# An encoder layer on one core: x^T laid out by the host, q rotated before the row scales are known

## The chip, the cores and the metric

The kernel runs on one core of one Trainium2 chip. The metric is the device time in microseconds (us), the median of several runs. Inputs are float32; each matrix product is made from two rounded parts of each factor, an upper part (hi) and a rest (lo), so that the products hold nearly full precision.

## The reference, cut to what matters

```python
h = rms_norm(x, norm_mix_pre)                     # x is [256, 2048]
proj = einsum('bsd,dc->bsc', h, w_in)             # 2048 x 10240
qa, ka, va, qn, kn, vn, gates = split(proj)
qa, ka = apply_rope(qa), apply_rope(ka)           # per token, per head of 128
oa = diff_attention(qa, ka, va, lam)              # softmax(q k^T / sqrt(128)), two maps per head
on = neighbourhood_attention(qn, kn, vn, na_rpb)
...
y = mixed @ w_out;  x = x + rms_norm(y, ...)      # then a squared-ReLU MLP, 2048 -> 8192 -> 2048
```

The norm divides each token (row of x) by the root of its mean square. Since that is one factor per token, it can be put on after the product: the kernel multiplies x times the gain with the weights, and puts the row scales on q, k and v later. The rotation (rope) is linear in its input, and the softmax of a score takes any factor of a query's row as its scale.

## The kernel before, in words

All of x's normed transpose, hT, stays in SBUF: 16 tiles of [128 channels, 256 tokens hi | 256 tokens lo]. The weights stream through in groups of 512 columns, and a group in four chunks of 1 MiB (four tiles of 128 rows each). `load` issues a chunk on the SP queue into a buffer "raw" (three of them, in turn); `split` makes hi on ScalarE (CAST, L115) and lo on VectorE (TENSOR_TENSOR, L116), in two halves, into three hi and three lo buffers. A raw buffer is free when the lo part is made, a hi or lo buffer when TensorE has used it.

`wgroup` makes 512 columns transposed, four PSUM banks of 128 columns (L191 for hi times both parts, L192 for lo times hi); `agroup` makes v, with tokens on partitions (L229 to L231). Four PSUM banks serve these in turn: a bank of q must be read out before k's can take it, a bank of k before v's. The first groups are q (qa), k (ka) and v (va) of the first two differential heads, then the same for the next two, and so on to the gates, the projections and the MLP. The order on each engine is made by a scheduler when the program is built.

At the start x comes in four blocks of [256 tokens, 512 columns], between the chunks of q's weight. `x_parts` transposes it on TensorE (L268, 32 transposes), and ScalarE and VectorE make hi and lo of it times the gain, from PSUM (L273, L274). `x_squares` sums the squares of each block on ScalarE (L345). `row_scales` then makes rx, the factor of each token: as a column, times 1/sqrt(128) (rxs), and, through two products with ones on TensorE (L78), as a row on all partitions (rxb), by which the tables cosT and sinT are multiplied. `rope_evac` adds the two halves of a bank (L254 on ScalarE copies one half, L256 on VectorE adds), which frees the bank, and rotates with the scaled tables (L385 to L388). So q, k and v all come out scaled. `diff_head` scores a head (ds) and applies the exponential with the scale 1/sqrt(128).

`small_inputs` loads the tables, the four lambda vectors (lq), subln, mask and g_mlp; before, it stands in the postlude, behind the last chunk of q. Loads take eight semaphores in turn, DMAHW0 to DMAHW7. A load that comes to one of them waits in the queue until the earlier load with it has landed, and all that stands behind it on SP waits too.

Of the kernel before, what the change touches and what calls it, by code (L numbers as in the profile page):

```python
# [14 lines left out]
ALU = mybir.AluOpType  # L15
# [23 lines left out]
def encoder_layer(ctx: ExitStack, tc: tile.TileContext, a, out):  # L39
# [32 lines left out]
    def along_tokens(r, b, name):  # L72
        """r [P tokens, token tile] as a row of all tokens, on all partitions."""
        ps = bank(f"{name}_p")
        for t in range(2):
            dg = t1k(f"{name}_d{t}")
            nc.vector.tensor_scalar_mul(dg[:, :P], ident, r[:, t : t + 1])
            nc.tensor.matmul(ps[:, t * P : (t + 1) * P], ones, dg[:, :P], start=True, stop=True)  # L78
        nc.scalar.copy(b, ps[:, :T])

    def inv_rms(ss, n, name, r=None):
        """(ss / n + eps) ** -0.5, per partition."""
# [9 lines left out]
    last_load = [None]  # L92

    def load(src, k0, nk, c0, cw, name):
        """Rows k0*128.. of a weight: [P, nk, cw]."""
# [5 lines left out]
    def split(raw, name, pieces=2, after=()):  # L101
        """Two float32r parts whose sum is raw. after[s] are instructions that go ahead of piece s."""
# [28 lines left out]
    x = a["x"]  # L131
    xv = x.rearrange("(t p) c -> p t c", p=P)
    xp = []
    first = []
    for i in range(4):
        xt = page([P, 2, 512], F32, f"x_{i}")
        xi = xv[:, :, i * 512 : (i + 1) * 512]
        xp.append(xt)
        if i == 0:
            raw = wp.tile([P, 4, 512], F32, tag="raw", name="first0_w")  # L140
            view = a["w_in"][: 4 * P, QA : QA + 512].rearrange("(k p) c -> p k c", p=P)
            for h in range(2):
                cs = slice(h * 256, (h + 1) * 256)
                nc.sync.dma_start(xt[:, :, cs], xi[:, :, cs])
                for k in range(h * 2, h * 2 + 2):
                    nc.sync.dma_start(raw[:, k], view[:, k])
            first.append(raw)
        else:
            nc.sync.dma_start(xt, xi)
            if i < 3:  # L150
                first.append(load(a["w_in"], i * 4, 4, QA, 512, f"first{i}"))
# [20 lines left out]
    def advance(n):  # L172
        """Trace the next n stages of the attention heads that wait for their turn, and one chore."""
# [9 lines left out]
    def wgroup(src, c0, act, nk, evac, name, first=(), hook=None, mid=None, after={}, k_first=False, inner=None):  # L183
        """out^T of 512 columns: weights stationary. act(k) is [P, hi 256 | lo 256]."""
# [35 lines left out]
    def agroup(src, c0, stat, nk, evac, name, tail=1, between=None):  # L220
        """out of 512 columns: activations stationary. stat(k, t) is (hi, lo) of [P, 128].
        The last ``tail`` chunks go token tile by token tile; between(i) may trace instructions
        ahead of the i-th of the second tile's products there and returns the last of them."""
# [27 lines left out]
    def halves(ps, name):  # L251
        """The sum of the two halves of a bank, in SBUF."""
# [7 lines left out]
    hT = [page([P, 2, 512], F32R, f"hT{i}") for i in range(8)]  # L260

    def x_parts(i):
        """The transpose of four tiles of x times the gain, in two parts [P, hi | lo]."""
        acts = []
        for k in range(i * 4, i * 4 + 4):
            pt = bank(f"hT_t{k}")
            for t in range(2):
                nc.tensor.transpose(  # L268
                    pt[:, t * P : (t + 1) * P], xp[i][:, t, (k % 4) * P : (k % 4 + 1) * P], ident
                )  # L270
            d = hT[k // 2][:, k % 2]
            g = g_pre[:, k : k + 1]
            acts.append(nc.scalar.activation(d[:, :T], pt[:, :T], AF.Copy, scale=g).ins)  # L273
            nc.vector.scalar_tensor_tensor(  # L274
                d[:, T:], pt[:, :T], g, d[:, :T].bitcast(F32), op0=ALU.mult, op1=ALU.subtract
            )

# [18 lines left out]
    ssx = const.tile([P, 8], F32, name="ssx")  # L296

# [22 lines left out]
    # Position bias: row (h, i) of rpbp holds the bias of row offset i - 3 at column offsets  # L320
    # -63..63. Each is written 64 times at a pitch of 127 and read at a pitch of 126.
# [20 lines left out]
    def x_squares(i):  # L342
        for t in range(2):
            j = junk512("jx0").rearrange("p a b -> p (a b)")
            nc.scalar.activation(  # L345
                j, xp[i][:, t], AF.Square, accum_out=ssx[:, t * 4 + i : t * 4 + i + 1]
            )

    def postlude():
        with tc.issue_after(last_load[0]):  # L350
            small_inputs()
        row_scales()
        head_constants()

    def prelude(ch):
# [3 lines left out]
        if ch >= 2:  # L359
            x_squares(ch - 2)  # L360
        if ch == 3:
            x_squares(2)
            x_squares(3)
        return [[]] + [acts[i : i + 1] for i in range(3)] if ch == 0 else None

# [8 lines left out]
    def product3(ps, stat, s_at, mov, m_at, start, stop):  # L374
        """ps (+)= stat^T @ mov, each given in two parts."""
# [43 lines left out]
    def p_transposed(p, name):  # L419
        """[P queries, (t, keys)] -> [P keys, (key tile, queries)]"""  # L420
# [12 lines left out]
    def diff_head(h, qT, kT, v, hl):  # L433
        p = t2k(f"dp{h}")
        for t in range(2):
# [16 lines left out]
            nc.vector.tensor_scalar_mul(nbs, nb, SCALE)  # L452
            e = t2k(f"de{h}{t}")
            z = small(2, f"dz{h}{t}")
            for c in range(2):
# [5 lines left out]
                    scale=SCALE,  # L461
# [108 lines left out]
    head = dict(first=first, hook=prelude, mid=postlude, k_first=True)  # L570
    for kind in ("a", "n"):
        for half in range(2):
# [7 lines left out]
            wgroup(w_in, kc + off, hmov, KD, kev(kT), f"k{nm}")  # L580
            agroup(w_in, vc + off, hstat, KD, v_evac(v), f"v{nm}")
            if kind == "a":
                pending += [diff_head(half * 2 + hl, qT, kT, v, hl) for hl in range(2)]
# [289 lines left out]
```

## Time and profile before

| | |
|---|---|
| median of three runs | 1396.07 us (1395.98 to 1398.43) |
| span of the profiled execution, first to last instruction | 1394.5 us |
| TensorE (PE) busy | 1374.6 us, 99% |
| VectorE (DVE) busy | 835.8 us, 60% |
| ScalarE (ACT) busy | 668.7 us, 48% |
| HBM traffic | 191 GB/s over the span |

The profiled execution has no time of its own beside the span; the span is 1.6 us under the median. Times in rows are us from the span's start. Matmuls overlap in the pipe: a row's length is that of one from its start to its modelled end, and the distance between starts is what one costs. In the list of waits the columns are: who waited, for whom, us in total, times, longest.

### The profile page before, as it was taken

The numbers are of one execution on the slowest core, as the hardware profiler recorded it, in microseconds if no ns is written. First come the engines' busy times: TensorE is split into PE (matmuls) and PEld (weight loads), VectorE is DVE, ScalarE is ACT, GpSimd is POOL, SyncE is SP. The second block draws the span as 40 slices with busy tenths as digits, with TensorE's granted clock in tenths as the row PEclk, the third lists the DMA queues.
The fourth block names the chain that finished last, engine by engine and source line by source line (L and its number), as shares of the span: only waits on it lengthen the run. The fifth ranks groups of instructions, "written<-read, shape, count | busy, mean of one in ns | idle before, by whom it ended". The sixth has DMA issues, their size and how long they took to land.

```text
span 1394.5 us, 17896 instructions
## 1 busy us (share of the span) xinstructions
PE 1374.6 (99%) x7240; PEld 1177.8 (84%) x7240; DVE 835.8 (60%) x1155; ACT 668.7 (48%) x1023; POOL 7.9 (1%) x19
## 2 busy tenths in 40 slices
PE   7999999999999999999899999999999999999997
PEld 6888888888888888888788888888888888888886
DVE  6868866676656565654755555555575554444445
ACT  7554554545444445543744444444464543334332
POOL 0000000000000000000000000000000000000000
PEclk9999999999999999999999999999999999999999
DMA  9674755564555555675455565656555556555551
GB/s 317 202 214 154 202 177 173 171 191 155 165 205 182 203 181 183 203 279 184 149 182 181 182 193 170 211 170 200 189 196 185 203 186 227 195 187 205 181 199 73
DMA packets 117490, 265.16 MB, mean 190 GB/s; under 512 B 15008, under 2 KB 16288, under 8 KB 109216
## 3 DMA queue, kind: packets, MB, share of 16 engines
q1 hardware_dynamic: 117264, 264.03, 57.3%
q8 instruction: 56, 0.92, 0.3%
q14 instruction: 26, 0.21, 0.0%
q10 hardware_dynamic: 144, 0.01, 0.0%
HBM read 261.92 MB, written 3.92 MB: 191 GB/s over the span
## 4 chain that ended last, share of the span: by engine, by line
PE 98%; DVE 1%; DMA 0%; ACT 0%; SPq 0%; issue 0%; DVEq 0%; POOLq 0%; POOL 0%; ACTq 0%
PE u_p L191 17%; PE u_p L192 9%; PE acc L779 8%; PE acc L778 8%; PE acc L777 8%; PE gb_p L191 4%; PE ga_p L191 4%; PE qa_p L191 2%; PE gb_p L192 2%; PE ga_p L192 2%; PE ka_p L191 2%; PE qn_p L191 2%; PE bb_p L191 2%; PE ba_p L191 2%; PE kn_p L191 2%; PE y_p L229 2%
## 5 line engine op out<-in xcount | busy, mean ns | idle before, releaser
L191 PE MATMUL u_p<-h2T,u_h 128*128 128x512 f32 x1024 | 359.9, 398 | 0.5 <-DVE r_m L85 0.5
L192 PE MATMUL u_p<-h2T,u_l 128*128 128x256 f32 x1024 | 284.3, 280 | 0.0
L116 DVE TENSOR_TENSOR d_l<-d_w,d_h 128x1024 fp32r<-128x1024 f32 x128 | 151.1, 1221 | 164.2 <-ACT d_h L115 163.7
L116 DVE TENSOR_TENSOR u_l<-u_w,u_h 128x1024 fp32r<-128x1024 f32 x128 | 151.1, 1222 | 146.0 <-ACT u_h L115 144.7
L191 PEld LDWEIGHTS u_p<-h2T,u_h 128*128 128x128 f32 x1024 | 192.0, 189 | 45.5 <-DVE r_m L85 0.9
L115 ACT CAST d_h<-d_w 128x1024 fp32r<-128x1024 f32 x128 | 128.3, 1052 | 191.1 <-PE acc L779 187.5
L778 PE MATMUL acc<-d_l,uh 128*128 128x512 f32 x512 | 199.0, 389 | 0.0
L779 PE MATMUL acc<-d_h,ul 128*128 128x512 f32 x512 | 198.9, 389 | 0.0
L777 PE MATMUL acc<-d_h,uh 128*128 128x512 f32 x512 | 198.2, 389 | 0.0
L192 PEld LDWEIGHTS u_p<-h2T,u_l 128*128 128x128 f32 x1024 | 193.8, 189 | 1.3
L115 ACT CAST u_h<-u_w 128x1024 fp32r<-128x1024 f32 x128 | 128.0, 1049 | 123.9 <-PE u_p L191 62.5
L778 PEld LDWEIGHTS acc<-d_l,uh 128*128 128x128 f32 x512 | 96.1, 188 | 20.1
L777 PEld LDWEIGHTS acc<-d_h,uh 128*128 128x128 f32 x512 | 96.1, 188 | 20.0
L779 PEld LDWEIGHTS acc<-d_h,ul 128*128 128x128 f32 x512 | 96.1, 188 | 19.8
L191 PE MATMUL gb_p<-hT,gb_h 128*128 128x512 f32 x256 | 90.4, 398 | 0.0
L191 PE MATMUL ga_p<-hT,ga_h 128*128 128x512 f32 x256 | 90.0, 397 | 0.0
L192 PE MATMUL gb_p<-hT,gb_l 128*128 128x256 f32 x256 | 71.4, 281 | 0.0
L192 PE MATMUL ga_p<-hT,ga_l 128*128 128x256 f32 x256 | 70.3, 280 | 0.0
L191 PEld LDWEIGHTS gb_p<-hT,gb_h 128*128 128x128 f32 x256 | 47.9, 188 | 11.5
L116 DVE TENSOR_TENSOR gb_l<-gb_w,gb_h 128x1024 fp32r<-128x1024 f32 x32 | 37.8, 1221 | 31.1 <-ACT gb_h L115 31.1
L191 PEld LDWEIGHTS ga_p<-hT,ga_h 128*128 128x128 f32 x256 | 47.4, 188 | 10.5
L116 DVE TENSOR_TENSOR y_l<-y_w,y_h 128x1024 fp32r<-128x1024 f32 x32 | 37.9, 1222 | 27.8 <-ACT y_h L115 27.8
(213 smaller groups left out, 2348.1 us busy)
## 6 DMA issues: line engine op xcount, KB each, us to landing
u_w<-in_w_up SPq DMA_DIRECT2D x64, 1024.0 KB, 5.4
d_w<-in_w_down SPq DMA_DIRECT2D x64, 1024.0 KB, 4.9
ga_w<-in_w_in SPq DMA_DIRECT2D x16, 1024.0 KB, 5.2
gb_w<-in_w_in SPq DMA_DIRECT2D x16, 1024.0 KB, 5.2
y_w<-in_w_out SPq DMA_DIRECT2D x16, 1024.0 KB, 5.1
ka_w<-in_w_in SPq DMA_DIRECT2D x8, 1024.0 KB, 6.1
va_w<-in_w_in SPq DMA_DIRECT2D x8, 1024.0 KB, 5.2
qn_w<-in_w_in SPq DMA_DIRECT2D x8, 1024.0 KB, 5.1
```

Of the source, the lines that this page charges most:

```text
L115: nc.scalar.copy(hi[part], raw[part])
L116: nc.vector.tensor_sub(lo[part], raw[part], hi[part].bitcast(F32))
L191: nc.tensor.matmul(ps[b], hi[:, k % 4, cs], mv, start=(k == 0), stop=False)
L192: nc.tensor.matmul(ps[b][:, :T], lo[:, k % 4, cs], mv[:, :T], start=False, stop=(k == nk - 1))
L229: nc.tensor.matmul(ps[t], sh, hi[:, k % 4], start=(k == 0), stop=False)
L777: nc.tensor.matmul(acc[t][c], uh[:, k % 4, ts_], hi[:, 0, cs], start=(k == 0), stop=False)
L778: nc.tensor.matmul(acc[t][c], uh[:, k % 4, ts_], lo[:, 0, cs], start=False, stop=False)
L779: nc.tensor.matmul(acc[t][c], ul[:, k % 4, ts_], hi[:, 0, cs], start=False, stop=(k == NK - 1))
```

## The change

The host gives x a second time, transposed and laid out as [128 channels, 16 tiles, 256 tokens] (xT). hT is made from it straight out of SBUF, without transposes. The loads at the start are cut into other pieces and put in the order in which TensorE uses them. x itself is now loaded in the k group, only for the squares; with that the row scales come at the end of the k group. q of the first two heads is rotated with the plain tables, and its scale goes into the exponential of these heads (rxs in place of the constant). k, v and all later groups have scaled tables as before.

```diff
-    for i in range(4):
-        xt = page([P, 2, 512], F32, f"x_{i}")
...
+    nc.sync.dma_start(first[0][:, 0], fv[0][:, 0])
+    nc.sync.dma_start(xT[0][:, 0:1], a["xT"][:, 0:1])
+    nc.sync.dma_start(first[0][:, 1], fv[0][:, 1])
+    nc.sync.dma_start(xT[0][:, 1:4], a["xT"][:, 1:4])
+    for k in range(2, 4):
+        nc.sync.dma_start(first[0][:, k], fv[0][:, k])
+    for i in range(1, 3):
+        nc.sync.dma_start(xT[i], a["xT"][:, i * 4 : i * 4 + 4])
+        for h in range(2):
+            nc.sync.dma_start(first[i][:, h * 2 : h * 2 + 2], fv[i][:, h * 2 : h * 2 + 2])
+    last_load[0] = nc.sync.dma_start(xT[3], a["xT"][:, 12:16]).ins
...
     def x_parts(i):
...
-            pt = bank(f"hT_t{k}")
-            for t in range(2):
-                nc.tensor.transpose(
-                    pt[:, t * P : (t + 1) * P], xp[i][:, t, (k % 4) * P : (k % 4 + 1) * P], ident
-                )
+            src = xT[i][:, k % 4]
...
-            acts.append(nc.scalar.activation(d[:, :T], pt[:, :T], AF.Copy, scale=g).ins)
+            acts.append(nc.scalar.activation(d[:, :T], src, AF.Copy, scale=g).ins)
...
+    def x_rows(i):
+        xt = page([P, 2, 512], F32, f"x_{i}")
+        nc.sync.dma_start(
+            xt, a["x"].rearrange("(t p) c -> p t c", p=P)[:, :, i * 512 : (i + 1) * 512]
+        )
+        xp.append(xt)
...
     def postlude():
-        with tc.issue_after(last_load[0]):
-            small_inputs()
         row_scales()
         head_constants()
...
-        if ch >= 2:
-            x_squares(ch - 2)
+        if ch == 2:
+            with tc.issue_after(last_load[0]):
+                small_inputs()
         if ch == 3:
-            x_squares(2)
-            x_squares(3)
+            with tc.issue_after(last_load[0]):
+                x_rows(0)
...
+    def second(ch):
+        if ch < 3:
+            with tc.issue_after(last_load[0]):
+                x_rows(ch + 1)
+        x_squares(ch)
...
-    def diff_head(h, qT, kT, v, hl):
+    def diff_head(h, qT, kT, v, hl, sc):
...
-            nc.vector.tensor_scalar_mul(nbs, nb, SCALE)
+            nc.vector.tensor_scalar_mul(nbs, nb, sc[t])
...
-                    scale=SCALE,
+                    scale=sc[t],
...
-    head = dict(first=first, hook=prelude, mid=postlude, k_first=True)
+    head = dict(first=first, hook=prelude, k_first=True)
+    head_k = dict(hook=second, mid=postlude)
...
-            wgroup(w_in, kc + off, hmov, KD, kev(kT), f"k{nm}")
+            wgroup(w_in, kc + off, hmov, KD, kev(kT), f"k{nm}", **(head_k if nm == "a0" else {}))
...
+                sc = [rxs[:, t : t + 1] for t in range(2)] if half == 0 else [SCALE] * 2
+                pending += [diff_head(half * 2 + hl, qT, kT, v, hl, sc) for hl in range(2)]
...
+        "xT": f["x"][0].T.reshape(KD, P, T).transpose(1, 0, 2),
```

On the SP queue, before, the fourth chunk of q's weight (qa_3_w) and the first of k's stand among the small inputs; a name in brackets is what a load waits for.

```order
L149 DMA x_105<-in_x 128x2x512 [waits DMAHW3_49]
L98 DMA qa_3_w<-in_w_in 128x4x512 [waits DMAHW5_49,DMAHW6_49,DMAHW4_49,DVE_49]
L160 DMA cosT<-in_cosT 128x256
L161 DMA sinT<-in_sinT 128x256
L164 DMA subln<-in_subln 128x2 [waits DMAHW7_49]
L165 DMA mask<-in_mask 128x64 [waits DMAHW0_49]
L166 DMA g_mlp<-in_g_mlp_pre 128x16 [waits DMAHW1_49]
L98 DMA ka_0_w<-in_w_in 128x4x512 [waits DMAHW2_49,DVE_49]
```

In the changed kernel the same stretch of the SP queue reads as follows; xT_92 is the last quarter of x^T, and sinT is the load that holds DMAHW7.

```order
L148 DMA xT_92<-in_xT 128x1024 [waits DMAHW5_49]
L157 DMA cosT<-in_cosT 128x256 [waits DMAHW6_49]
L158 DMA sinT<-in_sinT 128x256 [waits DMAHW7_49]
L160 DMA lq<-in_lam_q 128x128 [waits DMAHW0_49]
...
L161 DMA subln<-in_subln 128x2 [waits DMAHW4_49]
L162 DMA mask<-in_mask 128x64 [waits DMAHW5_49]
L163 DMA g_mlp<-in_g_mlp_pre 128x16 [waits DMAHW6_49]
L98 DMA qa_3_w<-in_w_in 128x4x512 [waits DMAHW7_49,DVE_49]
L98 DMA ka_0_w<-in_w_in 128x4x512 [waits DMAHW0_49,DVE_49]
L293 DMA x_299<-in_x 128x2x512 [waits DMAHW1_49]
L98 DMA ka_1_w<-in_w_in 128x4x512 [waits DMAHW2_49,DVE_49]
```

All nine small inputs now stand ahead of qa_3_w, and the first block of x (x_299) ahead of ka_1_w. Further on in the same queue the other three blocks of x stand behind the second chunk of v:

```order
L98 DMA va_0_w<-in_w_in 128x4x512 [waits DMAHW5_49,DMAHW2_49,DVE_49]
L98 DMA va_1_w<-in_w_in 128x4x512 [waits DMAHW6_49,DMAHW3_49,DVE_49]
L293 DMA x_389<-in_x 128x2x512
L293 DMA x_435<-in_x 128x2x512
L293 DMA x_481<-in_x 128x2x512 [waits DMAHW1_49]
L98 DMA va_2_w<-in_w_in 128x4x512 [waits DMAHW4_49,DVE_49]
```

Before, no load of x stood there. The wait of va_1_w for VectorE is for the raw buffer of ka_2.

On ScalarE, at the end of the k group and the start of v, before, the casts of the weights follow each other (qa_128 is q, rope_r the copied half of a bank):

```order
L371 CAST qa_128<-rope_s 128x256 x3
L115 CAST ka_3_h<-ka_3_w 128x1024 x2
L115 CAST va_0_h<-va_0_w 128x1024 x2
L115 CAST va_1_h<-va_1_w 128x1024 x2
L254 COPY rope_r<-ka_p_469 128x256
```

In the changed kernel the squares of the last blocks of x (jx, with the sum in ssx) stand between them:

```order
L301 ACTIVATE jx_483,ssx<-x_435 128x512
L301 ACTIVATE jx_485,ssx<-x_435 128x512
L115 CAST ka_3_h<-ka_3_w 128x1024 x2
L301 ACTIVATE jx_527,ssx<-x_481 128x512
L301 ACTIVATE jx_529,ssx<-x_481 128x512
L115 CAST va_0_h<-va_0_w 128x1024 x2
L115 CAST va_1_h<-va_1_w 128x1024 x2
```

On VectorE, before, the lo parts of the same chunks stood in one row ahead of the addition for k's first bank (ka_p_469). In the changed kernel the work on the row scales stands among them; ka_p_385 is k's first bank now, whose buffer v's first bank takes:

```order
L116 TENSOR_TENSOR ka_3_l<-ka_3_w,ka_3_h 128x1024 x2
L307 TENSOR_REDUCE sx<-ssx 128x2
L85 TENSOR_SCALAR rx_m<-sx 128x2
L319 TENSOR_REDUCE ls<-lv 128x2
L116 TENSOR_TENSOR va_0_l<-va_0_w,va_0_h 128x1024
L77 TENSOR_SCALAR rxb_d_553<-ident,rx 128x128
L77 TENSOR_SCALAR rxb_d_556<-ident,rx 128x128
L310 TENSOR_SCALAR rxs<-rx 128x2
L116 TENSOR_TENSOR va_0_l<-va_0_w,va_0_h 128x1024
L116 TENSOR_TENSOR va_1_l<-va_1_w,va_1_h 128x1024 x2
L322 SCALAR_TENSOR_TENSOR lam<-le 128x1
L253 TENSOR_TENSOR rope_s<-ka_p_385,rope_r 128x256
```

What moved here is the sum of the squares and what hangs on it (sx to rxs): before, it stood in the q group. On TensorE the two products for rxb stand between the last product of k and the first of v.

## Rows read from the trace of the kernel before

**Rows 1.** The page: span, and TensorE's busy time and instructions.
```profile
span 1394.5 us, 17896 instructions
...
PE 1374.6 (99%) x7240; PEld 1177.8 (84%) x7240; DVE 835.8 (60%) x1155; ACT 668.7 (48%) x1023; POOL 7.9 (1%) x19
```

**Rows 2.** TensorE's waits over the whole span.
```profile
PE hT_t L268 <- DMA x<-in_x: 6.0, 2, 3.9
```

**Rows 3.** TensorE in order of time: start, length, line, operation, tiles.
```profile
9.41 0.79 PE L191 MATMUL qa_p<-hT,qa_h 128*128 128x512 f32 x1 [1.20 <-DVE hT L274]
...
12.13 1.17 PE L268 MATMUL hT_t<-ident,x 128*128 128x128 f32 x6
...
36.58 0.39 PE L191 MATMUL ka_p<-hT,ka_h 128*128 128x512 f32 x1
...
58.89 0.40 PE L229 MATMUL va_p<-va_h,hT 128*128 128x512 f32 x1
59.13 0.40 PE L230 MATMUL va_p<-va_l,hT 128*128 128x512 f32 x1
```

**Rows 4.** SP's queue in order of time: start and length of a load's issue.
```profile
7.02 1.49 SPq L149 DMA_DIRECT2D x<-in_x  x1
12.39 0.37 SPq L98 DMA_DIRECT2D qa_w<-in_w_in  x1
...
13.35 0.43 SPq L161 DMA_DIRECT2D sinT<-in_sinT  x1
...
22.31 0.34 SPq L163 DMA_DIRECT2D lq<-in_lam_k  x1
22.76 0.38 SPq L98 DMA_DIRECT2D ka_w<-in_w_in  x1
...
25.54 0.38 SPq L98 DMA_DIRECT2D ka_w<-in_w_in  x1
...
34.16 0.37 SPq L98 DMA_DIRECT2D va_w<-in_w_in  x1
```

**Rows 5.** Loads by issue, same order, without 22.31: KB, us from issue to landing.
```profile
x<-in_x SPq DMA_DIRECT2D x1, 512.0 KB, 11.6
qa_w<-in_w_in SPq DMA_DIRECT2D x1, 1024.0 KB, 9.0
...
sinT<-in_sinT SPq DMA_DIRECT2D x1, 128.0 KB, 9.0
...
ka_w<-in_w_in SPq DMA_DIRECT2D x1, 1024.0 KB, 6.7
...
ka_w<-in_w_in SPq DMA_DIRECT2D x1, 1024.0 KB, 6.6
...
va_w<-in_w_in SPq DMA_DIRECT2D x1, 1024.0 KB, 5.1
```

**Rows 6.** ScalarE in order of time: a square's activation, two halves of a cast.
```profile
19.69 0.63 ACT L345 ACTIVATE jx<-x 128x512 f32<-128x512 f32 x1
...
30.68 2.00 ACT L115 CAST ka_h<-ka_w 128x1024 fp32r<-128x1024 f32 x2 [1.05 <-PE qa_p L191]
```

**Rows 7.** VectorE in order of time: diagonal tiles, a chunk's lo halves, a bank's addition.
```profile
22.63 0.47 DVE L77 TENSOR_SCALAR rxb_d<-ident,rx 128x128 f32<-128x128 f32 x2
...
49.23 2.36 DVE L116 TENSOR_TENSOR ka_l<-ka_w,ka_h 128x1024 fp32r<-128x1024 f32 x2 [1.83 <-ACT ka_h L115]
...
56.72 0.41 DVE L256 TENSOR_TENSOR rope_s<-ka_p,rope_r 128x256 f32<-128x256 f32 x1
```

**Rows 8.** TensorE around its wait in mid-kernel; a stretch with granted clock behind POOL's.
```profile
672.31 1.12 PE L664 MATMUL h2T_t<-ident,x 128*128 128x128 f32 x4 [3.18 <-DVE x L657]
673.96 0.79 PE L191 MATMUL u_p<-h2T,u_h 128*128 128x512 f32 x1 [0.53 <-DVE r_m L85]
...
678.18 0.53 PE L191 MATMUL u_p<-h2T,u_h 128*128 128x512 f32 x1
...
672.00:675.00 3.00, 2.15 (x7) 1.66 (x8) 2.88 (x10) 2.10 (x7) 0.54 (x1) 0.50 0.00 0
```

More of the change, by code (lines that the diff above doesn't have):

```diff
@@ L130, in encoder_layer @@
     nc.gpsimd.memset(ones, 1.0)
[L131 to L134, printed above, removed]
-    for i in range(4):
-        xt = page([P, 2, 512], F32, f"x_{i}")
[L137 to L151, printed above, removed]
+    xT = [page([P, 4, T], F32, f"xT{i}") for i in range(4)]
+    first = [wp.tile([P, 4, 512], F32, tag="raw", name=f"first{i}_w") for i in range(3)]
+    fv = [
+        a["w_in"][i * 4 * P : (i + 1) * 4 * P, QA : QA + 512].rearrange("(k p) c -> p k c", p=P)
+        for i in range(3)
+    ]
+    nc.sync.dma_start(first[0][:, 0], fv[0][:, 0])
[9 more added lines that the diff above has]
+    last_load[0] = nc.sync.dma_start(xT[3], a["xT"][:, 12:16]).ins
     g_mlp = const.tile([P, KD], F32, name="g_mlp")
@@ L265, in x_parts @@
         for k in range(i * 4, i * 4 + 4):
-            pt = bank(f"hT_t{k}")
-            for t in range(2):
-                nc.tensor.transpose(
-                    pt[:, t * P : (t + 1) * P], xp[i][:, t, (k % 4) * P : (k % 4 + 1) * P], ident
-                )
+            src = xT[i][:, k % 4]
             d = hT[k // 2][:, k % 2]
             g = g_pre[:, k : k + 1]
-            acts.append(nc.scalar.activation(d[:, :T], pt[:, :T], AF.Copy, scale=g).ins)
+            acts.append(nc.scalar.activation(d[:, :T], src, AF.Copy, scale=g).ins)
             nc.vector.scalar_tensor_tensor(
-                d[:, T:], pt[:, :T], g, d[:, :T].bitcast(F32), op0=ALU.mult, op1=ALU.subtract
+                d[:, T:], src, g, d[:, :T].bitcast(F32), op0=ALU.mult, op1=ALU.subtract
             )
@@ L296, in encoder_layer, with x_squares @@
     ssx = const.tile([P, 8], F32, name="ssx")
+    xp = []
+    def x_rows(i):
[4 more added lines that the diff above has]
+        xp.append(xt)
+    def x_squares(i):
+        for t in range(2):
+            j = junk512("jx0").rearrange("p a b -> p (a b)")
+            nc.scalar.activation(
+                j, xp[i][:, t], AF.Square, accum_out=ssx[:, t * 4 + i : t * 4 + i + 1]
+            )
     def row_scales():
@@ L340, in position_bias @@
         bias.append(bt)
[L342 to L347, printed above, removed]
     def postlude():
-        with tc.issue_after(last_load[0]):
-            small_inputs()
         row_scales()
@@ L579, in encoder_layer @@
             wgroup(w_in, qc + off, hmov, KD, qev(qT), f"q{nm}", **(head if nm == "a0" else {}))
-            wgroup(w_in, kc + off, hmov, KD, kev(kT), f"k{nm}")
+            wgroup(w_in, kc + off, hmov, KD, kev(kT), f"k{nm}", **(head_k if nm == "a0" else {}))
             agroup(w_in, vc + off, hstat, KD, v_evac(v), f"v{nm}")
             if kind == "a":
-                pending += [diff_head(half * 2 + hl, qT, kT, v, hl) for hl in range(2)]
+                sc = [rxs[:, t : t + 1] for t in range(2)] if half == 0 else [SCALE] * 2
+                pending += [diff_head(half * 2 + hl, qT, kT, v, hl, sc) for hl in range(2)]
             else:
@@ L636, in encoder_layer @@
             nc.sync.dma_start(
-                x2[t * 2 + h], x[t * P : (t + 1) * P, h * 1024 : (h + 1) * 1024]
+                x2[t * 2 + h], a["x"][t * P : (t + 1) * P, h * 1024 : (h + 1) * 1024]
             )
```

## The prediction, before the run

> **What bounds the kernel now.** I read the page first. The span is 1394.5 us and TensorE is busy for 1374.6 of them [rows 1]. Then I read TensorE's list of waits: it waits 6.0 us for x at the start [rows 2] and 3.2 us in the middle [rows 8], and else hardly at all. So only what makes TensorE start earlier, do less, or wait anew can show. The timeline gives the marks: first product of q at 9.41, the k group from 36.58, the v group from 58.89 [rows 3]. From 9.41 to 58.89 it has no wait worth a row. The question is therefore when the v group starts afterwards, since from there on the order is that of before.
>
> **What the change removes on TensorE.** The 32 transposes leave the stream. Six of them took 1.17 us at 12.13 [rows 3]; the 24 behind 9.41 are worth something between nothing and 4.7 us (24 at that rate). The first product needs one 256 KB piece of weight and 128 KB of x^T instead of x, a transpose and an evacuation. TensorE's longest wait for the first 256 KB was 3.9 us [rows 2]; with half that again to land and a cast and a subtraction behind it, q starts at 5.5 to 6.5 instead of 9.41. Taken alone that is 3 to 8 us. I do not take it, because the weights do not come that early.
>
> **Loads on SP up to k.** x^T and three quarters of q's weight are 5 MiB, as x and the same weight were. In the trace the last of these lands at 7.02 + 11.6 = 18.6, and the weight of q's last quarter, issued at 12.39 while the queue was still full, at 21.4 [rows 4, 5]. In the new order qa_3_w stands behind cosT, sinT, the four lambda vectors, subln, mask and g_mlp, and it waits for the semaphore that sinT holds, so for sinT's landing. That such a wait ends with the landing shows in the trace: the last lambda load, which shares a semaphore with sinT there, was issued at 22.31, when sinT landed [rows 4]. sinT landed 13.35 + 9.0 = 22.35, 0.95 behind the block ahead of it [rows 4, 5], so now 18.6 + 0.95 = 19.55. By then the queue is empty. A 1 MiB load on an empty queue took 5.1 (issued 34.16) [rows 4, 5]: qa_3_w lands at 24.7, 3.3 later than before.
>
> The Trainium skill's DMA: Bandwidth & Descriptors (Anatomy of one DMA) fits a GpSimd-issued load as 2.0 us plus bytes over 436 GB/s, 4.4 us for 1 MiB. By that everything below would come 0.7 us earlier, and my sum would be 1397.7; the row says 5.1 for this queue, and I keep it.
>
> Behind it come ka_0_w, the first block of x (512 KB, new here) and ka_1_w. In a full queue 1 MiB took 2.7: ka_1_w landed at 22.76 + 6.7 = 29.46 and ka_2_w at 25.54 + 6.6 = 32.14 [rows 4, 5]. So ka_0_w lands at 27.4, x block 0 at 28.75 and ka_1_w at 31.45, 2.0 later than before, for a TensorE that is ready for it 5 us earlier (below).
>
> **TensorE through q and k.** Half of qa_3's cast (1.0) and of its subtraction (1.2) [rows 6, 7] end at 26.9. A k group takes 58.89 - 36.58 = 22.3 [rows 3], so a quarter 5.6, of which about 1.0 runs on the upper parts alone before: q ends at 31.6, 5 ahead of before. Then k waits. ScalarE casts half of ka_1 from 31.45, copies q's first bank (0.4) and casts the other half, up to 33.8. VectorE subtracts the first half (1.2), adds the bank (0.4) and subtracts the second half: 35.2. Two rope products and the addition for q's second bank, 0.42 each, end at 36.5 and free the bank that k's second bank takes. TensorE stands there about 1.7 us and goes on at 36.5; 19.3 of k's 22.3 us are left, and with the 0.4 for the row scales it is ready for v at 56.2.
>
> **The x blocks and the squares.** VectorE goes on with half of ka_2 (1.2), three rope operations (1.3) and the other half: 40.1. That frees the raw buffer for which va_1_w waits on SP, and the last three x blocks stand behind va_1_w. It is issued at 40.2, lands at 45.3, and the blocks at 46.65, 48.0 and 49.35 (1.35 each, half of 2.7). On ScalarE the squares of blocks 1 and 2 stand ahead of ka_3's cast, those of block 3 ahead of va_0's. Two squares are 1.25 [rows 6]: ka_3's cast starts at 49.25. In the trace it was free of x, with all squares done inside q.
>
> From there VectorE sets the pace. First half of ka_3 cast at 50.25; subtraction 2.36 [rows 7], to 52.6; the sum of squares, the mean and the lambda sum 0.65 (three small ones, bounds 0.3 and 1.2); half of va_0 from 53.5 to 54.7; the two diagonal tiles and rxs 0.5 (a pair took 0.47 [rows 7]); the other half 1.2; va_1 2.36, to 58.75; lam and the addition for k's first bank 0.55. That addition frees the PSUM bank of v: **59.3**. In the trace the same addition began at 56.72 [rows 7], 1.8 before v needed it. So v starts 0.4 later than before, after a wait of 3.1 us (from 56.2). What else moves stays covered: v's second bank is freed at 63.8 (va_2's subtraction, then five operations of 0.42) and wanted 29 products later, at 66 (0.24 apart [rows 3]); va_3's cast is ready at 73, after some twenty more such operations, and wanted after 72 products, at 76.
>
> **The clock.** One gap like this stands in the trace: 3.18 us before 672.31. The granted clock is 0.50 in the stretch behind it, which is 1.2 GHz, and the first quick product stands at 678.18, 4.2 us after the first of its group at 673.96 [rows 8]. Half of 4.2 us, 2.1, is lost then; nothing if the clock holds. I take 1.9, near the upper end, since the row nearest to this wait shows the fall.
>
> The other edits cost nothing: hT is made from SBUF instead of PSUM, on engines that have done with each quarter before TensorE comes to it; rxs instead of a constant in two heads' exponentials changes an operand; the squares are moved, not added; 2 MiB more of x is in the sum above.
>
> **Sum.** 1396.07 + 0.4 + 1.9 = 1398.4. The profiled execution spans 1394.5, 1.6 below the median shown, so its span would be 1396.8. What a measurement of this kernel can tell from no change is about 0.2%, 2.8 us.
>
> **Rivals.**
> - The clock holds over the gap (say because loads run a little faster and the gap is 2.5): the sum is 1396.07 + 0.4 or a few tenths less, 1396.3. For it: the trace has no shorter gap that shows a fall. Against: 3.1 and 3.18 are close.
> - The weights are not late. If qa_3_w and ka_1_w land 3 us or more earlier, because x^T's longer rows move faster or small loads free their semaphores sooner, the chain from 31.45 to 59.3 moves with them, until q's end holds it (30.3 at best: 5.5, 22.3, and 2.5 for the slow clock and a short wait at the start; its first bank is complete some 2 us before). Then k's second bank is free at 32.1 instead of 36.5 and v starts at 54.9 to 56.3, with a shorter gap and a full clock: 1392.1 to 1393.5, taken as 1392.8. Against: 5 MiB landed at 18.6 through the same queue, which was full.
> - Slower. The place is ScalarE at ka_3's cast, which waits for x block 2. Every us by which that block lands later than 48.0 delays v by one us, with the clock falling for certain. From 48.5 on the loss passes 2.8; at 49.0 it is 1.4 + 2.1, 1399.6. For it: three blocks and a weight share the queue there, and in a full queue loads took 6.6 and 6.7 rather than 5.1 [rows 5].
> - Out of reach is the plain gain of over 3 us; it needs qa_3_w and ka_1_w by 24 and 29.
>
> **Chances.** Forecast 0.37, clock holds 0.24, weights early 0.16, slower 0.23. Faster by over 0.2% comes only from the third (0.13), slower from the fourth with a little of the first (0.25), the rest is within. The range leaves out the far half of the third and the end of the fourth: 1393.4 to 1400.2; the forecast's own is 1397.2 to 1399.2.
>
> **What would show it.** Right: q's first product at 5.5 to 6.5; a hole in the loads near 20 to 22; qa_3_w issued near 19.6; ka_1's cast waiting for its load at 31; ka_3's cast waiting for x near 48; TensorE waiting for VectorE's addition about 3 us before v, and a granted clock of 0.5 behind it. Wrong: qa_3_w issued before 18, or k's wait list without VectorE.

## The result, and the profile of the changed kernel

The changed kernel takes 1398.99 us (median of 20 runs, 1398.06 to 1400.67), the kernel before 1397.49 us (20 runs beside it, 1395.98 to 1398.71). The ratio is 1.0013, its 95% interval 1.0007 to 1.0019: 1.8 us slower by the ratio, which is inside the 0.2% that was called no change. The three runs shown ahead of the prediction lay 1.4 us under the median of the 20.

The page of the changed kernel answers to [rows 1]: TensorE does the same 1374.6 us of work in 32 products fewer, in a span that is 4.3 us longer.

```profile
span 1398.8 us, 17839 instructions
...
PE 1374.6 (98%) x7208; PEld 1176.6 (84%) x7208; DVE 836.0 (60%) x1155; ACT 669.6 (48%) x1023; POOL 7.9 (1%) x19
```

TensorE's waits over the whole span (who waited, for whom, us in total, times, longest). Against [rows 2], the wait for x has become one for hT, and two waits have come in:

```profile
PE qa_p L188 <- DVE hT L267: 7.1, 2, 5.6
...
PE va_p L226 <- DVE rope_s L253: 2.0, 1, 2.0
PE ka_p L188 <- DVE rope_s L253: 2.0, 1, 2.0
```

TensorE in order of time (start, length, line, operation, in brackets the idle time before and who ended it) answers to [rows 3]:

```profile
5.57 0.80 PE L188 MATMUL qa_p<-hT,qa_h 128*128 128x512 f32 x1 [5.57 <-DVE hT L267]
...
10.08 2.08 PE L188 MATMUL qa_p<-hT,qa_h 128*128 128x512 f32 x4 [1.58 <-DVE hT L267]
...
35.47 0.51 PE L188 MATMUL ka_p<-hT,ka_h 128*128 128x512 f32 x1 [2.01 <-DVE rope_s L253]
...
58.42 0.60 PE L78 MATMUL rxb_p<-rxb_d,ones 128*128 128x128 f32 x4
61.06 0.50 PE L226 MATMUL va_p<-va_h,hT 128*128 128x512 f32 x1 [2.04 <-DVE rope_s L253]
...
62.65 0.63 PE L226 MATMUL va_p<-va_h,hT 128*128 128x512 f32 x1
...
65.99 0.40 PE L228 MATMUL va_p<-va_h,hT 128*128 128x512 f32 x1
```

q starts 3.84 us earlier than before; k starts 1.11 earlier, v 2.17 later. Between 62.65 and 65.64 the products of v stand 0.43 us apart instead of 0.23: the clock had not fallen when v went on, and fell some 1.4 us later. The stretches with the granted clock (the number ahead of the last two) say the same:

```profile
60.00:63.00 3.00, 1.94 (x7) 1.58 (x8) 2.97 (x5) 2.77 (x5) 0.00 (x0) 0.91 0.96 343
63.00:66.00 3.00, 3.00 (x9) 2.33 (x8) 2.89 (x8) 0.00 (x0) 0.00 (x0) 0.52 0.81 266
```

Behind both new waits stands the same kind of row. SP's queue (start of an issue) answers to [rows 4], ScalarE to [rows 6], VectorE to [rows 7]:

```profile
10.83 0.33 SPq L158 DMA_DIRECT2D sinT<-in_sinT  x1
...
19.72 0.38 SPq L98 DMA_DIRECT2D qa_w<-in_w_in  x1
...
21.29 10.42 SPq L98 DMA_DIRECT2D ka_w<-in_w_in  x3
...
41.94 1.82 SPq L293 DMA_DIRECT2D x<-in_x  x3
```

```profile
25.17 2.00 ACT L115 CAST qa_h<-qa_w 128x1024 fp32r<-128x1024 f32 x2 [4.65 <-DMA qa_w<-in_w_in]
...
32.78 1.05 ACT L115 CAST ka_h<-ka_w 128x1024 fp32r<-128x1024 f32 x1 [1.44 <-DMA ka_w<-in_w_in]
...
50.08 0.63 ACT L301 ACTIVATE jx<-x 128x512 f32<-128x512 f32 x1 [0.19 <-DMA x<-in_x]
...
51.33 1.98 ACT L115 CAST ka_h<-ka_w 128x1024 fp32r<-128x1024 f32 x2
```

```profile
35.00 0.42 DVE L253 TENSOR_TENSOR rope_s<-qa_p,rope_r 128x256 f32<-128x256 f32 x1
...
57.12 3.49 DVE L116 TENSOR_TENSOR va_l<-va_w,va_h 128x1024 fp32r<-128x1024 f32 x3
60.52 0.15 DVE L322 SCALAR_TENSOR_TENSOR lam<-le 128x1 f32<-128x1 f32 x1
60.59 0.41 DVE L253 TENSOR_TENSOR rope_s<-ka_p,rope_r 128x256 f32<-128x256 f32 x1
```

The additions at 35.00 and 60.59 read out the first bank of q and of k; k's and v's first products follow them by half a us. The first stands behind ka_1's cast, which waits for its load. The second stands behind the lo halves of v's weights, these behind ka_3's cast, and that behind the squares of x block 2, which wait for their load (50.08).

qa_3_w was late as forecast, but in this profile TensorE does not wait for it: from 10.08 to the end of q it has no wait worth a row.

### The profile page after: what moved, and what is told of

It reads as the page before. It is cut to its first block, busy times and chain, and to the rows that moved or that the text cites. A ratio compares the mean times of both kernels' runs of the same rounds, so it can differ in the third digit from the quotient of the medians.

```text
span 1398.8 us, 17839 instructions
## 1 busy us (share of the span) xinstructions
PE 1374.6 (98%) x7208; PEld 1176.6 (84%) x7208; DVE 836.0 (60%) x1155; ACT 669.6 (48%) x1023; POOL 7.9 (1%) x19
## 4 chain that ended last, share of the span: by engine, by line
PE 96%; DMA 2%; DVE 1%; ACT 0%; issue 0%; SPq 0%; DVEq 0%; POOLq 0%; POOL 0%; ACTq 0%
PE u_p L188 17%; PE u_p L189 9%; PE acc L787 8%; PE acc L785 8%; PE acc L786 8%; PE gb_p L188 4%; PE ga_p L188 4%; PE ga_p L189 2%; PE gb_p L189 2%; PE qn_p L188 2%; PE bb_p L188 2%; PE ba_p L188 2%; PE kn_p L188 2%; PE y_p L227 2%; PE y_p L226 2%; PE y_p L228 2%
```

## The experiments

All of them are meant to change only what comes up to v's start, so two marks tell most: when v's first product starts, and how long TensorE waited ahead of it. These come from one profile of each kernel. Times are medians of 5 to 11 runs (20 of the changed kernel); ratios are to the kernel before on the same chip, with 95% intervals, estimated from all runs and not from the two medians. The kernels ran on several chips, on which the median of before lay between 1396.84 and 1397.49.

| run | v starts | wait ahead of v | time | ratio |
|---|---|---|---|---|
| before (profile shown) | 58.89 | none | 1397.2 | |
| changed kernel (profile shown) | 61.06 | 2.0, clock falls | 1398.99 | 1.0013 (1.0007 to 1.0019) |
| after_again | 59.75 | 2.0, clock falls | 1398.30 | 1.0009 (1.0001 to 1.0018) |
| e1_small_back | 59.25 | 1.9, clock falls | 1397.36 | 0.9999 (0.9990 to 1.0008) |
| d_pool_queue | 57.82 | 0.2 | 1395.44 | 0.9986 (0.9977 to 0.9995) |
| e4_no_rows | 57.2 | none | 1395.01 | 0.9989 (0.9980 to 0.9998) |
| e2_x_early | 60.15 | none | 1396.53 | 0.9995 (0.9986 to 1.0004) |
| v_first | 58.7 | none | 1396.36 | 0.9995 (0.9986 to 1.0004) |
| qv_first | 57.1 | none | 1393.96 | 0.9978 (0.9969 to 0.9987) |
| split | 54.0 | none | 1392.02 | 0.9963 (0.9951 to 0.9976) |
| best2 | 54.2 | none | 1391.74 | 0.9959 (0.9946 to 0.9971) |
| warm | 61.3 | 2.0, clock holds | 1399.20 | 1.0014 (1.0005 to 1.0022) |
| xT_alone | 63.0 | none | 1400.32 | 1.0020 (1.0012 to 1.0029) |
| best1 | 69.4 | none | 1406.24 | 1.0061 (1.0047 to 1.0075) |

Span less the start of v is 1335.6 in the profile of before, 1334.8 to 1336.1 in the ten profiles without a fall of the clock behind v, and 1337.4 to 1337.7 in the three with one (the changed kernel's two and e1_small_back). So a us at v's start is a us of the span, to about 0.7 either way. The fall costs 1.3 to 2.9 by these spans, about 1.8. The rows give it more closely: v's sixteenth product starts 5.17 us after the first in the changed kernel, and 3.54 after it in warm, where the wait was as long and the clock held (first at 61.29). That is 1.6 us.

```profile
66.23 0.39 PE L226 MATMUL va_p<-va_h,hT 128*128 128x512 f32 x1
```

```profile
64.83 0.39 PE L230 MATMUL va_p<-va_h,hT 128*128 128x512 f32 x1
```

### The changed kernel again

> The changed kernel once more, for a second profile and for times beside the other kernels on the same chip. Its times stood in two groups, 1398.1 to 1399.4 and 1399.9 to 1400.7, and the profile was taken from an execution of the upper one. Theory: the granted clock falls behind the 2 us wait ahead of v in the upper group alone. A profile near 1398.5 then shows v at 61 as well, but its products 0.24 apart all along; one near 1400.5 shows 0.43 for some 3 us. Rival: the clock falls in both, and the groups differ somewhere else.

This profile spans 1397.2, and its clock falls too:

```profile
59.75 0.50 PE L226 MATMUL va_p<-va_h,hT 128*128 128x512 f32 x1 [2.03 <-DVE rope_s L253]
```

```profile
60.00:63.00 3.00, 3.00 (x9) 2.31 (x9) 2.97 (x5) 1.35 (x4) 0.00 (x0) 0.56 0.77 254
```

The theory falls: this profile is of an execution of the lower group (1398.93), so the fall of the clock does not tell the two groups of times apart. The two profiles differ from the start on: the load of tiles 1 to 3 of x^T, issued at 2.11 in both, took 6.1 us in the first and 4.9 in this one.

```profile
xT<-in_xT SPq DMA_DIRECT2D x1, 384.0 KB, 6.1
```

```profile
xT<-in_xT SPq DMA_DIRECT2D x1, 384.0 KB, 4.9
```

So the second wait for hT ends at 8.88 instead of 10.08, qa_3's cast starts at 23.66 instead of 25.17, and all behind it is some 1.3 earlier; the spans differ by 1.6. Whether this load also makes the two groups of times, two profiles cannot show.

### Where the small inputs stand

e1_small_back puts them behind qa_3_w; d_pool_queue has GpSimd issue them at the start.

```diff
-        if ch == 2:
-            with tc.issue_after(last_load[0]):
-                small_inputs()
...
-    head = dict(first=first, hook=prelude, k_first=True)
+    head = dict(first=first, hook=prelude, mid=behind_q, k_first=True)
```

> The changed kernel with the small inputs (tables, lambda vectors, subln, mask, g_mlp) issued behind qa_3_w again instead of ahead of it; the scheduler then also puts the last three x blocks ahead of va_1_w. Theory (the loads pace q and k, and the x blocks with their squares pace v): qa_3_w lands near 21.5 instead of 25.1 and q loses nothing to it; ka_0_w takes over the wait for the semaphores and lands near 27, ka_1_w near 31 instead of 32.7; x block 2 near 43 instead of 49.6, so ka_3's cast no longer waits for squares; v starts near 56.5, no fall of the clock behind it, 1394.5 to 1395.5. Rival A (the late x blocks alone cost the time, the place of qa_3_w nothing): v starts where VectorE comes free, near 58, 1396.5. Rival B (the bubble only moves from q to k): ka_1_w still at 32 to 33, k's second bank at 36, v not before 58.9, 1397 to 1398.

Rival B came true: qa_3's cast starts at 21.40 and q's last product at 30.69, but ka_0_w now waits for the small loads, its cast starts at 28.56 and ka_1's at 32.96. The last x block is there at 48.4, and v starts at 59.25 after 1.9 us of waiting. The late load has only been handed on to k.

```diff
-        nc.sync.dma_start(cosT, a["cosT"])
+        nc.gpsimd.dma_start(cosT, a["cosT"])
```

(and so for the other eight)

> The changed kernel with the small inputs issued by GpSimd at the start instead of by SP between x^T and qa_3_w; SP's queue then holds the weights and x alone, with the last three x blocks ahead of va_1_w. Theory: nothing on SP waits for sinT, qa_3_w lands near 21.5 and ka_1_w near 28.5; q ends near 30.5 and k goes on with at most 0.5 of waiting; x block 2 lands before 43; v starts at 53.5 to 55.5 and the clock holds: 1393 to 1394.5. Rival (the small loads, now beside the first weights, take from these what they gave back, or the weights are no earlier because the queue is full): first product of q later than 6.5 or ka_1_w after 31, v at 57 or later, 1396 and more.

The loads went the rival's way. Nothing waits for sinT, and qa_3_w is issued at 12.30, but it takes 12.8 us and lands at 25.1, when it landed in the changed kernel too. ka_1_w lands at 31.9. The small loads took from the first ones what they gave back.

```profile
12.30 0.37 SPq L98 DMA_DIRECT2D qa_w<-in_w_in  x1
```

```profile
qa_w<-in_w_in SPq DMA_DIRECT2D x1, 1024.0 KB, 12.8
```

Still TensorE waits neither ahead of k nor (but for 0.2) ahead of v, since the scheduler read out q's first bank ahead of ka_1's cast here and put the last three x blocks ahead of va_1_w. Tiles 1 to 3 of x^T come as late as in the changed kernel, and q runs at the low clock until 16.1:

```profile
10.34 2.08 PE L188 MATMUL qa_p<-hT,qa_h 128*128 128x512 f32 x4 [2.08 <-DVE hT L267]
```

q ends at 34.4, and v starts at 57.82 instead of 53.5 to 55.5. The time lies between the two that were expected.

### The x blocks

> The changed kernel without the four loads of x and without the eight squares; the sums of squares are a constant instead, so the row scales are left out in effect. The small inputs stay ahead of qa_3_w. Theory: ka_1_w lands 1.35 earlier, near 31.4, the wait in k shrinks from 2.0 to 0.7, ka_3's cast follows its load, VectorE frees v's first bank before TensorE wants it, v starts near 57 without a wait and without a fall of the clock: 1395 to 1396, 3 to 4 under the changed kernel. Rival (VectorE's own work from 35 to 60 sets v, the x blocks are only the last to be seen): v still waits, near 60, and the time stays within 1.5 of the changed kernel's 1399.

```diff
-        x_squares(ch)
+        pass
...
+    nc.gpsimd.memset(ssx, 512.0)
```

The time is the theory's, and so is the step: ka_3's cast starts at 46.24, 5.1 earlier than in the changed kernel's profile and 3.8 earlier than in after_again, whose x^T came as early as here. v waits for nothing. For k the expectation was wrong: ka_1's cast starts at 30.33, 2.4 and 1.2 earlier, and yet k's first product waits 3.0 us:

```profile
31.41 2.36 DVE L116 TENSOR_TENSOR ka_l<-ka_w,ka_h 128x1024 fp32r<-128x1024 f32 x2 [0.32 <-ACT ka_h L115]
33.69 0.42 DVE L253 TENSOR_TENSOR rope_s<-qa_p,rope_r 128x256 f32<-128x256 f32 x1
```

```profile
34.16 0.50 PE L188 MATMUL ka_p<-hT,ka_h 128*128 128x512 f32 x1 [3.01 <-DVE rope_s L253]
```

The addition for q's first bank stands behind both lo halves of ka_1 here. So the wait in k is one of order, not of the load alone.

```diff
-                x_rows(0)
+                for i in range(4):
+                    x_rows(i)
...
-        if ch < 3:
-            with tc.issue_after(last_load[0]):
-                x_rows(ch + 1)
```

> The changed kernel with all four x blocks directly behind ka_0_w, ahead of ka_1_w; the small inputs stay ahead of qa_3_w. By the step on the x blocks (ka_3's cast waits for x block 2): that wait is gone, the squares end near 37. The price: ka_1_w lands three blocks, 4.05, later, near 36 to 36.7, so k's first product, behind q's first bank, behind ka_1's cast, starts near 38 to 39.5. Theory: VectorE has the same work from there but no waits of 1.6 and 2.3 on late squares, k ends near 61 to 62 and v starts there with less than 1 us of waiting; the clock falls behind the longer wait in k instead: 1399 to 1401, no gain. Rival (x blocks 2 and 3 alone set v): v at 58 to 59, 1396 to 1397.

Neither came true in full; the time is the rival's, the step is not. v starts at 60.15, between the two profiles of the changed kernel, but after no wait, and the clock holds. The time is 1.8 us under after_again, about what the fall costs. The price that I named did not come, since the scheduler now put the reading of q's first banks ahead of ka_1's cast (k starts at 35.09). ka_1 was missed later instead, and k ended later.

### The order in which banks are read

v_first lets va_1's cast and subtraction go behind the copy and the addition for k's first bank; qv_first lets ka_1's go behind those for q's first bank too.

```diff
+            va = {1: adds[4]} if nm == "a0" else {}
-            agroup(w_in, vc + off, hstat, KD, v_evac(v), f"v{nm}")
+            agroup(w_in, vc + off, hstat, KD, v_evac(v), f"v{nm}", after=va)
```

> The changed kernel with one order edit: the copy and the addition that read out k's first PSUM bank go ahead of the cast and the subtraction of va_1 on ScalarE and VectorE, where they stood behind them. Theory (the 2.0 us wait ahead of v is a queue: the bank is complete near 54, but its readers stand behind four casts and three subtractions of v's weights, which start late since x blocks 2 and 3 are late): the addition comes near 58.3 instead of 60.6, v starts when k and the row scales are done, near 59 (57.7 in the faster of the two profiles), no wait, and the clock does not fall behind it: 2 to 3.5 under the changed kernel, 1395.5 to 1396.5. Rival A (the readers are late because of k's own end or the row scales): v still near 60 to 61, 1398. Rival B (va_1 is then missed 5 us later): v starts at 59 but waits for va_1's parts near 64, 1397 to 1398.5.

The addition stands at 58.20, v starts at 58.7, right behind k and the row scales, and does not wait:

```profile
58.20 0.42 DVE L255 TENSOR_TENSOR rope_s<-ka_p,rope_r 128x256 f32<-128x256 f32 x1
```

The time is 1.9 under after_again, at the near end of what the theory gave. With the loads as they were and only this order changed, the wait is gone: the wait ahead of v was a queue on VectorE.

```diff
-            wgroup(w_in, kc + off, hmov, KD, kev(kT), f"k{nm}", **(head_k if nm == "a0" else {}))
+            wgroup(w_in, kc + off, hmov, KD, kev(kT), f"k{nm}", **(dict(head_k, after={1: adds[0]}) if nm == "a0" else {}))
```

> As v_first, and q's first bank is read out ahead of ka_1's cast and subtraction too. Theory for k: q's first bank is complete near 29, its copy and addition then come near 31.5 instead of 34 to 35, so k's first product follows q's last without the 2.0 to 2.4 us wait; ka_1 is wanted 1.4 us later and then holds k for 0.5 to 1.5 instead; ka_3's cast still waits for x block 2 near 50 and becomes what k waits for. Net gain over v_first 0 to 1: 1394.5 to 1396. Rival (k's wait was the whole of it, everything behind moves up with it): 2 under v_first, 1393.5 to 1394. Second rival (the wait in k only moves and grows): no better than v_first.

This is 2.4 better than v_first, the rival's time. k waits as the theory said, three times half a us, but ka_3 does not hold it, since the scheduler also moved the x blocks ahead of va_1_w. So the order of q's first bank takes the 2.5 us wait at k's start away, but how much of the 2.4 it earns without the earlier blocks was not measured.

```profile
32.62 0.50 PE L188 MATMUL ka_p<-hT,ka_h 128*128 128x512 f32 x1 [0.52 <-DVE rope_s L255]
35.02 0.39 PE L189 MATMUL ka_p<-hT,ka_l 128*128 128x256 f32 x1 [0.51 <-DVE ka_l L116]
36.49 0.38 PE L189 MATMUL ka_p<-hT,ka_l 128*128 128x256 f32 x1 [0.49 <-DVE ka_l L116]
```

### Weights first, and both

split puts only cosT and sinT behind qa_3_w and the rest of the small inputs behind ka_1_w; best2 is split with the orders of qv_first.

```diff
+    def behind_q():
+        with tc.issue_after(last_load[0]):
+            small_inputs()
...
+        if ch == 2:
+            with tc.issue_after(last_load[0]):
+                rest_inputs()
```

> The changed kernel with the two reading orders of qv_first, and with the small inputs taken apart: cosT and sinT behind qa_3_w, the others behind ka_1_w and later; the scheduler then puts x blocks 1 to 3 ahead of va_0_w. Theory (what is left in qv_first, v at 57.1, comes from qa_3_w behind sinT's landing, then ka_1_w): qa_3_w lands near 21.5, ka_0_w near 25, ka_1_w near 29; q ends near 30.7 and k follows at once; v starts at 53.5 to 55, 1390.5 to 1392.5, 1.5 to 3.5 under qv_first. Rival A (the end of q does not move, because the wait for x^T and the low clock at the start hold it): qa_3_w early, but q ends at 32 and v near 56, 1393. Rival B (VectorE's own work between 30 and 57 sets v): v stays near 57 with a wait ahead of it, 1394.

> As best2, but with the reading orders of the changed kernel. Theory (with the weights early, the readers stand behind casts that are no longer late, so the order matters less): k's first product waits under 1 us, v starts at 54.5 to 56.5 with a wait under 1 us, 1392 to 1394, at most 1.5 over best2. Rival (the reading order is the cause by itself, whatever the loads do): k and v wait 2 us each as in the changed kernel, v near 58, with the clock falling behind it, 1395 to 1396.5.

Both theories hold for the times; v comes even a little earlier in split than expected (54.0). In best2 qa_3's cast starts at 21.13 and ka_1's at 29.81, and k follows q without a wait:

```profile
30.37 0.28 PE L191 MATMUL qa_p<-hT,qa_l 128*128 128x256 f32 x1
30.49 0.40 PE L190 MATMUL ka_p<-hT,ka_h 128*128 128x512 f32 x1
```

split is the same within the intervals. But it does not have the reading orders of the changed kernel, as the expectation says: with the weights early the scheduler put the copy for q's first bank ahead of ka_1's cast by itself.

```profile
28.00 0.35 ACT L253 COPY rope_r<-qa_p 128x256 f32<-128x256 f32 x1
29.73 2.00 ACT L115 CAST ka_h<-ka_w 128x1024 fp32r<-128x1024 f32 x2 [1.37 <-DVE rope_u L397]
```

Only the order for k's first bank differs between the two: split reads it out behind va_1, at 52.8, best2 ahead of it, at 51.3, and both are early enough for v at 54. So with early weights that order is worth nothing more, and whether early weights would do without the order for q's bank was not tested. In both profiles q also ran at the full clock from the second tile on, which it did not in the changed kernel's; e1_small_back and qv_first had that too and gained less, so it is not enough by itself, but its share was not told apart. best2 is 0.41% faster than before (interval 0.29 to 0.54%), 5.1 us by medians; the same change has this gain in it when its loads stand in this order.

### TensorE's clock at the start

```diff
+    warm = bank("warm")
+    for i in range(12):
+        nc.tensor.matmul(warm[:, :P], ones, ones, start=True, stop=True)
```

> The changed kernel with twelve products of ones into an unused PSUM bank ahead of q's first product, so that TensorE works from about 1 us on; they compute nothing that is used. In the two profiles of the changed kernel q's products stood 0.43 us apart (1.2 GHz) until 13 to 14 us, in other kernels of this study until 8.9 to 9.7. Theory: the products stand 0.24 apart soon after the first one, q ends 2 to 3 earlier, near 29.5 to 31, but k's first product still waits for ka_1's cast and q's first bank, 34.2 to 35.5, so v starts as before, 59.8 to 61: the same time within 0.7, 1398 to 1399. Rival (the low clock at the start is what ate the earlier start): v moves up by the same 2 to 3, 1395.5 to 1396.5.

The theory holds for the time and for v; the end of q, which it put at 29.5 to 31, came at 32.5. q's products run at the full clock after the first: from 6.75 to 7.09 are 0.34 us, for one product of 512 columns and one of 256:

```profile
1.17 5.39 PE L134 MATMUL warm<-ones 128*128 128x128 f32 x24 [1.17 <-POOL ones L130]
6.31 0.48 PE L192 MATMUL qa_p<-hT,qa_h 128*128 128x512 f32 x1
...
6.75 0.40 PE L192 MATMUL qa_p<-hT,qa_h 128*128 128x512 f32 x1
...
7.09 0.40 PE L192 MATMUL qa_p<-hT,qa_h 128*128 128x512 f32 x1
```

But q then waits 1.5 us for qa_3 up to 26.4, and k 2.4 us up to 35.08, and v starts at 61.3. A faster q buys nothing while the loads and the bank's readers hold k.

### x^T without the later row scales

```diff
-    head = dict(first=first, hook=prelude, k_first=True)
-    head_k = dict(hook=second, mid=postlude)
+    head = dict(first=first, hook=prelude, mid=postlude, k_first=True)
+    head_k = dict(hook=second)
```

(and all x blocks and squares in q's fourth chunk, the constant scale in the exponentials)

> The changed kernel with x^T from the host and its loads in the order of use, but the row scales where they were before: all four x blocks behind ka_0_w, their squares within q, the row scales at the end of q, q rotated with scaled tables, the constant scale in the exponentials. Theory: the row scales need all of x, which lands near 34; ScalarE's squares stand ahead of the copy of q's first bank and of ka_1's cast, ka_1_w lands near 36 to 37, and TensorE's products for the row scales wait for the squares: k starts 3 to 6 later than in the changed kernel, at 38 to 41, v at 61.5 to 64: 1399 to 1403, so the later row scales are what lets x^T come out even. Rival (the squares' place does not matter, since k's first product waits for ka_1 anyway): k near 36.5, v near 59, 1396.5 to 1397.5.

This is as the theory said. TensorE waits 5.3 us for the row scales ahead of k, and the clock falls in that wait:

```profile
37.14 1.23 PE L78 MATMUL rxb_p<-rxb_d,ones 128*128 128x128 f32 x4 [5.32 <-DVE rxb_d L77]
```

```profile
39.00:42.00 3.00, 3.00 (x11) 2.52 (x10) 3.00 (x5) 2.57 (x5) 0.00 (x0) 0.50 0.59 182
```

So the two halves of the change belong together: the later scales save 1.3 to 2 us of what x^T alone loses. The nearer comparison is e2_x_early on the same chip, whose x blocks stand at the same place and whose scales come late: there it is 3.8 us (1400.32 against 1396.53).

### A miss: the squares on GpSimd

```diff
+        nc.gpsimd.tensor_tensor(sq, xT[i], xT[i], op=ALU.mult)
+        nc.gpsimd.tensor_tensor(acc, acc, sq, op=ALU.add)
```

> The changed kernel with four edits: x itself is not loaded, the squares of x^T are summed on GpSimd and over the channels by two products with ones on TensorE; the small inputs stand behind qa_3_w; the first banks of q and of k are read out ahead of ka_1 and va_1. Theory: q ends near 30.5, k follows with at most 1 us of waiting for ka_1, the row scales are ready long before the end of k, v starts at 53.5 to 55 without a wait and the clock holds: 1391.5 to 1393.5. Rival A (GpSimd's sums are slow or slow VectorE down, and the two products with ones wait for them in TensorE's queue): a wait of several us between q and k, 1395 and more. Rival B (after v the time saved is lost again because the weights of the next groups come no earlier): v early, but a new wait before 100 us, 1394.5 and more.

Rival A came true in its first half: VectorE slows down by a factor of about four while GpSimd works (8 to 28 us). The wait that follows stands within q, though, not between q and k. Four instructions for hT took 1.67 us in the changed kernel and 7.48 here:

```profile
11.87 1.67 DVE L267 SCALAR_TENSOR_TENSOR hT<-xT,g_pre,hT 128x256 fp32r<-128x256 f32 x4
```

```profile
18.20 7.48 DVE L269 SCALAR_TENSOR_TENSOR hT<-xT,g_pre,hT 128x256 fp32r<-128x256 f32 x4
```

TensorE waits 7.3 us, up to 27.93, for a lo part of q's weight, and v starts at 69.4.

## Why the prediction was right, and where it was not

The forecast was no change, by a chain of seven steps. Its outcome held, and so did the waits that it named, for k on a bank and for v on VectorE's addition. Of its steps one stood at the wrong place, one had the wrong cause, and two were mis-sized.

- **q's start, and the loads up to qa_3_w**: as forecast (5.5 to 6.5; 5.57 measured). sinT landed at 19.53 (19.55), qa_3_w was issued at 19.72 (19.55) and took 5.4 us on the empty queue (5.1), so it landed at 25.1 (24.7). The estimate of 4.4 us worked out from the Trainium skill's DMA: Bandwidth & Descriptors (Anatomy of one DMA), whose fit is for loads issued by GpSimd, did not show here.
- **The end of q**: 33.3 instead of 31.6, and for another reason. The forecast let qa_3_w set it; in both profiles of the changed kernel TensorE has no wait worth a row for that weight. It was late by itself: by the wait for tiles 1 to 3 of x^T (1.58 and 0.58) and by the low clock, at which the products run until 14.5 (12.5 in after_again) and not until 12 to 13 as before.
- **ka_1_w**: cast at 32.78 instead of 31.45. The x block ahead of it took 2.2 us in the queue, not 1.35.
- **"The bank that k's second bank takes"** is the step that failed. TensorE stood at k's first product, for q's first bank; no product of k was done before that wait. The prediction's own sum has that bank added only at 34.05 (33.65 + 0.4), and yet it counts 3.0 us of k (22.3 less 19.3) as done before a wait that begins at 34.8. So TensorE went on at 35.47 (36.5 was forecast) with all 22.3 us ahead of it, and was ready for v at 59.0, not 56.2. e4_no_rows and qv_first show that this wait hangs on the order on ScalarE and VectorE.
- **x block 2 and ka_3's cast**: the mechanism is right (e2_x_early and e4_no_rows take the wait away), its size 0.8 to 2.1 off: the block's squares start at 48.77 and 50.08 in the two profiles, not at 48.0. That is the condition of the slower rival. Its price, one us of v for each us of that block, gives 60.1 and 61.4; measured 59.75 and 61.06.
- **The wait ahead of v**: VectorE's addition, as forecast, 2.0 us instead of 3.1, since TensorE came later too. That the error of 2.8 us on k did not reach the time is luck: VectorE was later still.
- **The clock**: it fell, as forecast, and cost 1.6 (by the rows of v; about 1.8 by the spans) against 1.9 forecast.

By profiles v came 0.9 to 2.2 later, not 0.4, and with the clock the sum is +2.7 to +4.0 instead of +2.3 (the spans differ by 2.7 and 4.3). By medians it was +1.5. The profile shown of before is one of its faster executions (with the 1.8 us that lie between a span and its time, 1396.3, against a median of 1397.2 to 1397.5), and both profiles of the changed kernel are of executions above their medians (1400.62 against 1398.99, 1398.93 against 1398.30). So the sum of the forecast is nearer to the time than its steps are to the profiles. What moves before's time by 3 us from run to run was not examined. It is not a lower granted clock, as the column has it: of 33 runs on one chip, the 19 at a mean clock of 0.995 have a median of 1396.56, and the 14 at 0.996 one of 1398.10. The rival of early weights is what split and best2 made true: v at 54.0 to 54.2 (54.9 to 56.3 was forecast for it) and 1391.7 to 1392.0.

## What to carry to other kernels

When a stage is started earlier, follow what it will want next: here a start 3.8 us earlier was spent on a late piece of x^T, on a low clock, and on two PSUM banks whose readers stood in order behind casts of weights not yet landed. Small loads that share semaphores with large ones belong behind all the weights that are wanted first, and what frees a bank belongs ahead of what prepares data for later. By medians the reading orders gained 1.9 to 5.0 us on the changed kernel, the small loads taken apart, behind qa_3_w and behind ka_1_w, 6.3 to 7.0, all of them behind qa_3_w only 0.9 to 1.6, and the orders on top of the weights first no more. After each edit, look at the order that the scheduler built: here it often moved more than the edit asked for.

## What the runs showed of the hardware

- A wait of TensorE does not by its length decide whether the clock falls. It fell behind the wait ahead of v in three profiles (waits of 2.04, 2.03 and 1.85 us; changed kernel, after_again, e1_small_back), each time only after work had gone on: the granted clock of 60 to 63 us, 0.91, 0.56 and 0.54, puts the fall to 1.2 GHz some 1.4, 0.6 and 1.0 us behind v's first product. It fell within a wait of 5.3 us (xT_alone). It held behind 2.0 us ahead of v (warm) and behind 2.5 (v_first) and 3.0 (e4_no_rows) ahead of k. What decides was not settled.
- At the start q's products of 512 columns stood 0.43 us apart, where they stand 0.23 apart later, while the granted clock of these stretches read 1.00. So the products of the first tile of x^T ran at 1.2 GHz in all profiles of the changed kernel and its variants but warm, which had products ahead of q. Behind the wait that followed, six profiles ran at the full clock from the next tile on (from 8.9 to 9.7 us: e1_small_back, e4_no_rows, qv_first, split, best2, xT_alone), and the others at the low one until 12.5 to 18.3 us. Here the distance of the products tells the clock, not the column.
- GpSimd's element-wise work on 128x1024 tiles slowed VectorE's instructions for hT by a factor of 4.5 (7.48 against 1.67, best1). The Trainium skill's GPSIMD Engine Reference (Specifications) says that GpSimd shares its SBUF interfaces with VectorE and contends with instructions that take two inputs from SBUF. These rows take two (xT and hT), and agree.
